# Every third weight tile of an fp32r decoder trunk split by two GpSimd transfers instead of ScalarE and VectorE

## The chip, the core and the metric

The kernel runs on one core of a Trainium2 chip. Its engines are TensorE (PE in the rows; PEld is its weight load), VectorE (DVE), ScalarE (ACT), GpSimd (POOL) and SyncE (SP), with 16 DMA engines beside them. The metric is the device time of one execution in microseconds (us).

## What is computed

A two-layer decoder trunk over 256 tokens of width 1024 in float32. Each layer is a feed-forward block (FFN), a mixer, and a second FFN, each followed by a layer norm. Cut to its core:

```
for l in range(2):
    x = layer_norm(ALPHA*x + 0.5*swiglu(x, ffn_w_gu[l,0], ffn_w_down[l,0]))
    y = mixer_ab(x) if l % 2 == 0 else mixer_c(x)     # attention + gated MLP; mLSTM
    x = layer_norm(ALPHA*x + y)
    x = layer_norm(ALPHA*x + 0.5*swiglu(x, ffn_w_gu[l,1], ffn_w_down[l,1]))

def swiglu(x, w_gu, w_down):
    g, u = split(x @ w_gu, 2)
    return (silu(g) * u) @ w_down
```

FFN widths are 1024 to 2 x 2816 and 2816 back to 1024. Nearly all of the work is products with weights that are used once.

## The kernel before

The weights are packed into 324 tiles of 128 x 1024 float32 (512 KB), numbered in the order of use. Tiles 0 to 65 belong to the first FFN, 66 to 93 to `mixer_ab`, 94 to 159 and 160 to 225 to the second and third FFN, 226 to 257 to `mixer_c`, 258 to 323 to the last FFN. Tiles 0 to 3 come in another way, with x (in_F).

To keep float32 accuracy each operand is a pair: a high part rounded to float32r (`whi`, `xTh`) and a low part, the remainder (`wlo`, `xTl`). `mm3` (lines 119 to 122) multiplies high by high, high by low and low by high into the same PSUM tile.

A weight tile n passes three steps. `w_dma(n)` (line 73) loads it from HBM into one of RAW = 6 `raw` buffers, on SP's queue. `w_split(n)` (line 78) makes `whi` and `wlo`, each a ring of RING = 9 buffers: ScalarE casts `raw` to `whi` (line 92), VectorE subtracts `whi` from `raw` into `wlo` (line 93). Then TensorE uses the pair and `w_done(n)` (line 86) frees it. `w_done(n)` also writes the next steps into the program: `w_split(n + 9)`, whose cast must wait until TensorE has released tile n's buffers, and `w_dma(n + 15)`.

In the FFN, `proj_t` takes one tile per 128 columns of `x @ w_gu`: 24 matmuls of 256 columns into a PSUM bank `ps_m` (3 banks). `chunk` uses two tiles, gate and up: ScalarE's Silu reads the gate bank (line 334), VectorE multiplies with the up bank (line 337), and the product is split again into `hT`. `out_proj` multiplies `hT` with the last 22 tiles of an FFN, in 12 matmuls of 512 columns each, into `ps_a`.

`layer_norm` (line 206) runs on VectorE, except for one small step: GpSimd's power function (line 203, `lnrs`; the same line serves `sgrs` and `hrs` in the mixers). After it VectorE finishes the row block (line 226) and TensorE transposes it (line 234). GpSimd does little else than these powers.

SP's instructions run in the order of the program text. On the other engines a list scheduler chooses the order within an engine when the kernel is built; each engine then works strictly in that order, and an instruction that waits holds up all that stand behind it.

Of the kernel before, what the change touches and what calls it, by code (L numbers as in the profile page):

```python
# [7 lines left out]
F32 = mybir.dt.float32  # L8
# [3 lines left out]
OP = mybir.AluOpType  # L12
# [18 lines left out]
def trunk(ctx, tc, W, F_d, x_d, g_d, b_d, rope_d, id_d, idb_d, mk_d, tri_d, sel_d,  # L31
          sg_d, sb_d, sw_d, sbt_d, cw_d, wif_d, bif_d, hg_d, out_d):
    nc = tc.nc
    NG = W.shape[0] + 4
# [35 lines left out]

    raw, whi, wlo = {}, {}, {}

    def w_dma(n):
        if n < NG:
            raw[n] = wpool.tile([P, 1024], F32, tag="raw", name="raw", bufs=RAW)
            nc.sync.dma_start(out=raw[n], in_=W[n - 4])

    def w_split(n):
        if n < NG:
            hi = wpool.tile([P, 1024], F32R, tag="hi", name="whi", bufs=RING)  # L80
            lo = wpool.tile([P, 1024], F32R, tag="lo", name="wlo", bufs=RING)
            r = raw.pop(n)
            split(r, hi, lo)
            whi[n], wlo[n] = hi, lo

    def w_done(n):
        del whi[n], wlo[n]
        w_split(n + RING)
        w_dma(n + RING + RAW)

    def split(src, hi, lo):
        nc.scalar.copy(out=hi, in_=src)  # L92
        nc.vector.tensor_tensor(out=lo, in0=src, in1=hi.bitcast(F32), op=OP.subtract)  # L93
# [63 lines left out]
    def feed(i):  # L157
        if i < KC:
            st[i] = wpool.tile([P, 1024], F32, tag="raw", name="raw", bufs=RAW)
            eng = nc.scalar if i in (1, 3) else nc.sync  # L160
            eng.dma_start(out=st[i][:, 0:768], in_=F_d[i])
        else:
            w_dma(i - KC + 4)
# [22 lines left out]
    for n in range(4, RING):  # L186
        w_split(n)
        w_dma(n + RAW)
# [669 lines left out]
```

## Time and profile before

| | |
|---|---|
| median of 3 runs | 972.62 us (971.28 to 972.83) |
| profiled execution, its own time | 971.34 us |
| its span in the trace | 969.5 us |
| TensorE busy | 957.2 us, 99% of the span |
| VectorE busy | 599.0 us, 62% |
| ScalarE busy | 458.3 us, 47% |
| GpSimd busy | 25.1 us, 3% |
| SP's DMA queue (q1) | 181.25 MB, 57.4% of the 16 DMA engines' span |

The span lies between the first and the last instruction of the trace; the execution's own time is 1.84 us more. Busy shares are averages over stages with different limits. TensorE's granted clock was 0.999 of full speed.

### The profile page before, as it was taken

The page shows a single profiled execution, that of the slowest core. Times are in us where ns is not written, and L with a number is a line of the kernel's source. Part 1 is how long each engine was busy: PE and PEld are TensorE (multiplying, and loading weights), DVE is VectorE, ACT ScalarE, POOL GpSimd, SP SyncE. Part 2 cuts the span into 40 slices and gives each one's busy share as a digit, 9 for nine tenths or more (in the row PEclk, how much of TensorE's full clock was granted, in tenths as well). Part 3 has the DMA queues.
Part 4 walks back from the last instruction along what each step waited for, and adds up shares of the span by engine and source line. Part 5 has one row for each costly group of instructions (what it writes and reads, how often), then busy time and mean ns, then how long its engine had stood idle before and what let it go on. Part 6 is the DMA issues. An engine that isn't in the chain of part 4 may idle for free.

```text
span 969.5 us, 15552 instructions
## 1 busy us (share of the span) xinstructions
PE 957.2 (99%) x6210; PEld 856.0 (88%) x6210; DVE 599.0 (62%) x829; ACT 458.3 (47%) x669; POOL 25.1 (3%) x36
## 2 busy tenths in 40 slices
PE   8999999999999999999999999999999999999997
PEld 6999988887888999988889999888888789999886
DVE  7665544685777655544775555439767886555435
ACT  6554443446645444443354444325675445445320
POOL 0000000020100000000000000001000000000000
PEclk9999999999999999999999999999999999999999
DMA  9985656474436755656566666556643466665511
GB/s 344 327 273 189 194 177 193 157 273 157 131 130 217 235 182 193 190 183 193 173 225 188 194 183 190 190 157 218 217 125 123 135 218 233 189 194 184 187 44 43
DMA packets 51927, 183.01 MB, mean 189 GB/s; under 512 B 6160, under 2 KB 6544, under 8 KB 51728
## 3 DMA queue, kind: packets, MB, share of 16 engines
q1 hardware_dynamic: 51568, 181.25, 57.4%
q8 instruction: 48, 0.79, 0.3%
q10 hardware_dynamic: 288, 0.79, 0.2%
q14 instruction: 23, 0.19, 0.1%
HBM read 180.97 MB, written 1.05 MB: 188 GB/s over the span
## 4 chain that ended last, share of the span: by engine, by line
PE 70%; DVE 2%; POOL 0%; issue 0%; ACT 0%; DVEq 0%
PE ps_m L120 15%; PE ps_m L121 15%; PE ps_m L122 15%; PE ps_a L121 8%; PE ps_a L122 8%; PE ps_a L120 8%; DVE wlo L93 1%; PE ps_a L234 1%; POOL hrs L203 0%; PE ps_t L323 0%; ACT whi L92 0%; PE ps_a L499 0%; DVE hst L680 0%; DVE num L707 0%; PE ps_a L661 0%
## 5 line engine op out<-in xcount | busy, mean ns | idle before, releaser
L93 DVE TENSOR_TENSOR wlo<-raw,whi 128x1024 fp32r<-128x1024 f32 (+1 forms) x327 | 394.0, 1213 | 232.8 <-ACT whi L92 231.4
L92 ACT CAST whi<-raw 128x1024 fp32r<-128x1024 f32 (+1 forms) x327 | 339.7, 1042 | 380.0 <-PE ps_m L121 194.4
L120 PE MATMUL ps_m<-xTh,whi 128*128 128x256 f32 x1280 | 358.2, 280 | 1.4 <-DVE qkc L647 1.4
L121 PE MATMUL ps_m<-xTl,whi 128*128 128x256 f32 x1280 | 357.6, 279 | 0.0
L122 PE MATMUL ps_m<-xTh,wlo 128*128 128x256 f32 x1280 | 357.4, 279 | 0.0
L120 PEld LDWEIGHTS ps_m<-xTh,whi 128*128 128x128 f32 x1280 | 240.6, 188 | 2.1 <-ACT cch L92 1.6
L121 PEld LDWEIGHTS ps_m<-xTl,whi 128*128 128x128 f32 x1280 | 240.6, 188 | 0.4 <-issue 0.2
L122 PEld LDWEIGHTS ps_m<-xTh,wlo 128*128 128x128 f32 x1280 | 240.6, 188 | 0.3 <-issue 0.3
L121 PE MATMUL ps_a<-wlo,hT 128*128 128x512 f32 (+1 forms) x352 | 138.1, 392 | 0.0
L120 PE MATMUL ps_a<-whi,hT 128*128 128x512 f32 (+1 forms) x352 | 138.1, 392 | 0.0
L122 PE MATMUL ps_a<-whi,hT 128*128 128x512 f32 (+1 forms) x352 | 138.0, 392 | 0.0
L120 PE MATMUL ps_m<-whi,xTh 128*128 128x512 f32 x224 | 90.8, 405 | 0.0
L121 PE MATMUL ps_m<-wlo,xTh 128*128 128x512 f32 x224 | 89.3, 399 | 0.0
L122 PE MATMUL ps_m<-whi,xTl 128*128 128x512 f32 x224 | 88.7, 396 | 0.0
L120 PEld LDWEIGHTS ps_a<-whi,hT 128*128 128x128 f32 x352 | 66.1, 188 | 15.2
L122 PEld LDWEIGHTS ps_a<-whi,hT 128*128 128x128 f32 x352 | 66.1, 188 | 15.1
L121 PEld LDWEIGHTS ps_a<-wlo,hT 128*128 128x128 f32 x352 | 66.2, 188 | 15.0
L337 DVE TENSOR_TENSOR hp<-hp,ps_m 128x256 f32<-128x256 f32 x74 | 31.2, 422 | 52.9 <-PE ps_m L122 52.8
L122 PEld LDWEIGHTS ps_m<-whi,xTl 128*128 128x128 f32 x224 | 42.1, 188 | 9.6
L120 PEld LDWEIGHTS ps_m<-whi,xTh 128*128 128x128 f32 x224 | 42.2, 189 | 8.9
L121 PEld LDWEIGHTS ps_m<-wlo,xTh 128*128 128x128 f32 x224 | 42.2, 188 | 8.7
L212 DVE SCALAR_TENSOR_TENSOR xn<-xn,ps_a 128x512 f32<-128x512 f32 x24 | 16.0, 685 | 37.1 <-PE ps_a L122 37.0
(199 smaller groups left out, 609.2 us busy)
## 6 DMA issues: line engine op xcount, KB each, us to landing
raw<-in_W SPq DMA_DIRECT2D x320, 512.0 KB, 4.0
gb<-in_g SPq DMA_DIRECT2D x6, 512.0 KB, 4.0
gb<-in_b SPq DMA_DIRECT2D x6, 512.0 KB, 4.9
raw<-in_F SPq DMA_DIRECT2D x6, 384.0 KB, 4.2
xn<-in_x SPq DMA_DIRECT2D x1, 1024.0 KB
out<-xn SPq DMA_DIRECT2D x4, 256.0 KB, 2.0
raw<-in_F ACTq DMA_DIRECT2D x2, 384.0 KB, 5.2
swt<-in_sw SPq DMA_DIRECT2D x2, 256.0 KB, 7.4
```

Of the source, the lines that this page charges most:

```text
L92: nc.scalar.copy(out=hi, in_=src)
L93: nc.vector.tensor_tensor(out=lo, in0=src, in1=hi.bitcast(F32), op=OP.subtract)
L120: mm_(out=out, lhsT=lh, rhs=rh, start=start, stop=False)
L121: mm_(out=out, lhsT=lh, rhs=rl, start=False, stop=False)
L122: mm_(out=out, lhsT=ll, rhs=rh, start=False, stop=stop)
L212: nc.vector.scalar_tensor_tensor(out=sl, in0=sl, scalar=scale, in1=acc[i], op0=OP.mult, op1=OP.add)
L234: nc.tensor.transpose(pt[:, c, :], sl[:, c * P:(c + 1) * P], ident)
L337: nc.vector.tensor_tensor(out=hp[:, 1, :], in0=hp[:, 0, :], in1=pu, op=OP.mult)
```

## The change

Tiles n with n >= 12 and n divisible by 3 (104 of the 324) are split in another way. They have no `raw` buffer and no transfer on SP. GpSimd issues a transfer from HBM into `whi` whose destination type is float32r, so that the transfer rounds. ScalarE writes `wlo` = -`whi`. GpSimd then issues a second transfer of the same HBM tile into `wlo` that adds to what is there. VectorE has no part in these tiles.

```diff
+    def viadma(n):
+        return 12 <= n < NG and n % 3 == 0
+
     def w_dma(n):
-        if n < NG:
+        if n < NG and not viadma(n):
             raw[n] = wpool.tile([P, 1024], F32, tag="raw", name="raw", bufs=RAW)
             nc.sync.dma_start(out=raw[n], in_=W[n - 4])
 
     def w_split(n):
         if n < NG:
             hi = wpool.tile([P, 1024], F32R, tag="hi", name="whi", bufs=RING)
             lo = wpool.tile([P, 1024], F32R, tag="lo", name="wlo", bufs=RING)
-            r = raw.pop(n)
-            split(r, hi, lo)
+            if viadma(n):
+                nc.gpsimd.dma_start(out=hi, in_=W[n - 4])
+                nc.scalar.mul(out=lo, in_=hi.bitcast(F32), mul=-1.0)
+                nc.gpsimd.dma_start(out=lo, in_=W[n - 4], accum_op=OP.add)
+            else:
+                r = raw.pop(n)
+                split(r, hi, lo)
             whi[n], wlo[n] = hi, lo
```

How the instructions stand on two engines follows. Line numbers grow by 8 below the edit: 92 becomes 100, 203 becomes 211, 334 becomes 342. A number behind a name counts the buffers handed out; `wlo_1094` and `whi_1093` are one tile, and a higher number is a later tile.

GpSimd, from its set-up to the first two layer norms' powers, before the change:

```order
L138 MEMSET half_82 128x8
L139 MEMSET zero_81 128x256
L203 ISA
L203 TENSOR_TENSOR lnrs_2018<-lnrs_2018,half_82 128x1
L203 TENSOR_TENSOR lnrs_2144<-lnrs_2144,half_82 128x1
L396 MEMSET kp_2100 64x256
```

Nothing stands between the set-up and the powers: GpSimd waits for VectorE and no more.

GpSimd at the end of the first FFN after the change, around the first of these powers (the pairs shown here are the last of many):

```order
L86 DMA whi_1834<-in_W 128x1024
L88 DMA wlo_1835<-in_W 128x1024
L86 DMA whi_1887<-in_W 128x1024
L88 DMA wlo_1888<-in_W 128x1024
L211 ISA
L211 TENSOR_TENSOR lnrs_1994<-lnrs_1994,half_82 128x1
L86 DMA whi_1976<-in_W 128x1024
L86 DMA whi_2025<-in_W 128x1024
L88 DMA wlo_1977<-in_W 128x1024
L88 DMA wlo_2026<-in_W 128x1024
```

Between set-up and power there are now transfers. Those of a tile stand as a pair, high then low, and in the FFN the pairs follow one another strictly: the high part of the next such tile is behind the low part of the one before. A high transfer waits for TensorE's release of the buffer, a low one for ScalarE's negation. The powers now stand behind such pairs.

ScalarE, in the same `chunk` part; before:

```order
L92 CAST whi_901<-raw_701 128x1024
L92 CAST hT_908<-hp_843 128x256
L92 CAST whi_937<-raw_737 128x1024
L334 ACTIVATE hp_911<-ps_m_912 128x256
L92 CAST whi_969<-raw_769 128x1024
L92 CAST hT_976<-hp_911 128x256
```

and after:

```order
L100 CAST whi_1025<-raw_827 128x1024
L87 ACTIVATE wlo_995<-whi_994 128x1024
L100 CAST hT_1032<-hp_968 128x256
L100 CAST whi_1061<-raw_863 128x1024
L342 ACTIVATE hp_1035<-ps_m_1036 128x256
L100 CAST hT_1099<-hp_1035 128x256
L100 CAST whi_1128<-raw_930 128x1024
L87 ACTIVATE wlo_1094<-whi_1093 128x1024
L342 ACTIVATE hp_1102<-ps_m_1103 128x256
```

The negation of a tile (line 87) stands directly behind the cast of the tile after it, once in three tiles, and Silu and the splits of `hT` stand behind the negation.

## Rows read from the trace of the kernel before

**Rows 1.** The page's first part: span, and busy time of the engines.
```profile
span 969.5 us, 15552 instructions
PE 957.2 (99%) x6210; PEld 856.0 (88%) x6210; DVE 599.0 (62%) x829; ACT 458.3 (47%) x669; POOL 25.1 (3%) x36
```

**Rows 2.** TensorE in order of time in the first FFN: start, duration, instruction.
```profile
99.79 0.28 PE L120 MATMUL ps_m<-xTh,whi 128*128 128x256 f32 x1
99.91 0.28 PE L121 MATMUL ps_m<-xTl,whi 128*128 128x256 f32 x1
...
102.59 0.28 PE L120 MATMUL ps_m<-xTh,whi 128*128 128x256 f32 x1
```

**Rows 3.** Busy time by stage: FFN, mixer_ab, mixer_c; then clock, DMA share, GB/s.
```profile
66.60:122.60 56.00, 56.00 (x482) 56.00 (x482) 32.10 (x40) 26.92 (x42) 0.00 (x0) 1.00 0.59 188
191.00:290.00 99.00, 98.70 (x557) 79.51 (x556) 72.83 (x125) 54.88 (x109) 9.02 (x14) 1.00 0.53 176
666.00:770.00 104.00, 101.86 (x578) 86.05 (x577) 77.12 (x153) 57.44 (x90) 7.99 (x8) 1.00 0.47 154
```

**Rows 4.** ScalarE in order of time in the FFN; in brackets idle time before, releaser.
```profile
110.37 1.05 ACT L92 CAST whi<-raw 128x1024 fp32r<-128x1024 f32 x1 [1.44 <-PE ps_m L121]
111.32 0.38 ACT L334 ACTIVATE hp<-ps_m 128x256 f32<-128x256 f32 x1
113.17 1.05 ACT L92 CAST whi<-raw 128x1024 fp32r<-128x1024 f32 x1 [1.47 <-PE ps_m L121]
114.12 0.40 ACT L92 CAST hT<-hp 128x256 fp32r<-128x256 f32 x1
```

**Rows 5.** Groups by line and shape: count, busy us, mean ns, idle before.
```profile
L93 DVE TENSOR_TENSOR wlo<-raw,whi 128x1024 fp32r<-128x1024 f32 x320 | 389.2, 1224 | 232.7 <-ACT whi L92 231.4
L92 ACT CAST whi<-raw 128x1024 fp32r<-128x1024 f32 x320 | 335.4, 1051 | 380.0 <-PE ps_m L121 194.4 <-PE ps_a L122 149.9 <-PE ps_m L122 21.6
L203 POOL TENSOR_TENSOR lnrs<-lnrs,half 128x1 f32<-128x1 f32 x12 | 11.4, 951 | 803.0 <-DVE lnrs L202 789.3 <-DMA raw<-in_W 13.7
L203 POOL TENSOR_TENSOR hrs<-hrs,half 128x2 f32<-128x2 f32 x4 | 4.6, 1152 | 80.9 <-DVE hrs L202 80.9
L203 POOL TENSOR_TENSOR sgrs<-sgrs,half 128x1 f32<-128x1 f32 x2 | 3.1, 1554 | 52.1 <-DVE sgrs L202 52.1
```

**Rows 6.** The tile raw from 66 to 123 us: issue in ns, time to landing.
```profile
L76 SPq DMA_DIRECT2D raw<-in_W x20: 327/328/328, 67.9 to 121.1; - x20
...
DMA to landing us min/median/max: 3.3/3.5/4.2
```

**Rows 7.** The page's third part: SP's queue, packets, MB, share of 16 engines.
```profile
q1 hardware_dynamic: 51568, 181.25, 57.4%
```

**Rows 8.** Who waited for whom: total us, times, longest us.
```profile
PEld ps_a L234 <- DVE xn L226: 1.3, 6, 0.3
DVE hrs L701 <- POOL hrs L203: 2.8, 4, 0.8
```

## Prediction

> **What bounds the kernel now.** I read the busy times first. TensorE is busy for 957.2 of 969.5 us [rows 1], so at most 12.3 us of the span are not matmuls, whatever is done to the other engines. TensorE's own instructions are the same after the change, so these 12.3 us bound every gain. Next, in order of time, TensorE in an FFN: 24 matmuls of 256 columns lie between 99.79 and 102.59 us [rows 2], so one weight tile takes 2.80 us and three take 8.40. In the FFN window TensorE is never idle, while the DMA engines are used for 0.59 of the time at 188 GB/s [rows 3]. ScalarE shows who leads: each cast of a tile starts after an idle time of 1.44 us that ends when TensorE releases the buffer [rows 4]. The splitting keeps up easily; it runs at TensorE's pace with nine tiles, 25.2 us, from the release of a buffer to the next use.
>
> **The change part by part.** *Removed:* 104 subtractions on VectorE, 1.224 us each [rows 5], 127 us of an engine that TensorE does not wait for in the FFN: worth nothing there. In the mixers TensorE idles for 0.30 us of 99 and 2.14 us of 104 [rows 3], where VectorE is busier; freeing it can give back 2.4 us at most. I take 0.
>
> *Replaced:* 104 casts on ScalarE become 104 negations of the same size. No row shows the negation; its nearest row is the cast, 1.051 us [rows 5]. The bound below is Silu's 0.38 us for a quarter of the elements [rows 4], which would leave the sum nearly as it is. I take 1.05, so ScalarE's load stays.
>
> *Moved and added:* 104 raw transfers leave SP and 208 transfers of 512 KB appear on GpSimd. This is where the time is decided, because of the order on GpSimd and ScalarE. For one tile: GpSimd waits for the release, issues the high transfer, ScalarE waits for it to land, negates, GpSimd issues the low transfer, and only then, in GpSimd's order, can the high transfer of the next such tile be issued. That is a loop, and TensorE offers it 8.40 us per turn in an FFN. If the loop is longer, the ring's lead runs out and TensorE goes at the loop's pace.
>
> The loop's terms. (a) Issue on GpSimd, once for each transfer. Not shown: from below SP's issue, 0.33 us [rows 6]; from above GpSimd's longest mean for its own tiny instruction, 1.55 us [rows 5]. GpSimd takes 0.95 us even for 128 x 1 elements [rows 5], and I take 0.93, close to that: two issues are 1.9 us. (b) The high transfer from issue to landing. SP's take 3.3 to 4.2 us, median 3.5 [rows 6]. Of this the bytes are 1.65 us: 188 GB/s at a share of 0.59 is 319 GB/s at full use [rows 3], and a tile is 0.524 MB. Whether a rounding transfer is slower is not shown; below one pass, above two. I take one, 3.5 us. (c) The low transfer must read its destination as well as HBM. Bounds: one pass, 1.65 us, if the second read is free, and three, 4.95. I take two, 3.3 us of engine time. It was issued just before the next high transfer on the same queue, so that one stands behind it for 3.3 - 0.93 = 2.4 us. (d) Two raw transfers per loop, 3.3 us of the DMA engines, share them. The GpSimd transfers hold the engines for 4.95 us of a loop of some 10.5; the part of the raw work that falls into it is 3.3 x 4.95 / 10.5 = 1.6 us. (e) Negation 1.05 and two hand-overs, 0.1 together. Sum: 1.9 + 3.5 + 2.4 + 1.6 + 1.15 = 10.5 us against 8.40. That is 2.1 us per turn.
>
> No run here shows the price of an accumulating transfer. The Trainium skill, Collectives: The Full Stack, section The bandwidth ceiling: the fold count and why AG ≠ RS ≠ AR, says that an add inside a transfer halves its rate, because it needs two source reads and not because of the adding; by that (c) would be two passes.
>
> The four FFNs hold 84 such tiles (18 in the first, 22 in each other): 84 x 2.1 = 176 us. The lead absorbs some of it once: 25.2 us less a tile's unhindered way of 0.93 + 3.5 + 1.15 + 0.93 + 3.5 + 1.65 = 11.7 leaves 13.5 us. In the mixers three tiles take 99 / 28 x 3 = 10.6 us and 104 / 32 x 3 = 9.75 us [rows 3], so a loop of 10.5 neither costs nor rebuilds the lead in the first, and costs ten turns x 0.75 = 7.5 us in the second. 176 - 13.5 + 7.5 = 170 us.
>
> *The powers on GpSimd:* 18 of them [rows 5] now stand behind transfers that wait. Six transposes arrived at TensorE with only 0.2 us of waiting each [rows 8], that is, with no room left; VectorE in mixer_c waits for `hrs` already, 2.8 us in four [rows 8]. A power can be late by nothing, or by one high transfer, negation and issue, 0.93 + 3.5 + 1.15 = 5.6 us. At 2 us each that is 36 us; where TensorE waits for tiles anyway most of it lies under that, and I take 10.
>
> *Behind the waiting negation on ScalarE* stands Silu. TensorE needs that PSUM bank again two tiles, 5.6 us, after filling it. The negation stands behind the next tile's cast, at 2.8 + 1.05 = 3.9 us after the release; with an unhindered landing after 4.4 us this costs nothing, with 6.8 us (with the wait behind the low transfer) Silu still makes it. The loop binds first.
>
> *DMA engines:* SP's 57.4% [rows 7] lose 104 x 0.524 = 54.5 of 181.25 MB, 17.3 points; the high transfers put 17.3 back and the low ones add 34.5: 92% of the old span, 892 us, so bandwidth alone is not the bound.
>
> The profiled execution took 971.3 us: 971.3 + 170 + 10 = 1151; the median of the runs is 1.3 higher: 1152 us.
>
> **The rivals.** *Hidden (15%).* If the low transfer costs one pass and the issue 0.33 us, the loop is 0.66 + 3.5 + 1.3 + 1.3 + 1.15 = 7.9 us, below 8.40, and TensorE never notices: 971 to 975 us. TensorE's 99% and the 41% of free DMA time speak for it [rows 1, 3]; it decides at 8.40. The Trainium skill, DMA: Bandwidth & Descriptors, section Anatomy of one DMA — SWDGE (gpsimd) path, fits a GpSimd transfer as 2.0 us plus its bytes at 436 GB/s; that estimate gives 3.2 us for a tile, issue and landing together, and would bring the hidden case. No row of this trace has a transfer from GpSimd.
>
> *The loop fits, the powers are late (12%).* 18 x 1 to 2 us on top: 990 to 1010 us. For it speak the transposes without room [rows 8].
>
> *Transfers that compute are slow (12%).* With three passes for the low and two for the high one, and 1.55 us for an issue, (a) to (e) give 3.1 + 5.15 + 3.4 + 1.9 + 1.15 = 14.7 us: 84 x 6.3 plus about 90 in the mixers, less the lead, some 600 us more: 1580. Against it speaks only that nothing shows it.
>
> *Faster (6%).* VectorE without a third of its subtractions lets TensorE's 2.4 us of waits in the mixers go: 969 to 970 us. This needs a loop under 8.40 us and powers on time.
>
> **How the numbers follow.** The loop as summed has 55%. Its own range is from a loop just over 8.40 us, with the powers late, 1000 us, to three passes for the low transfer: (c) 4.0, (d) 2.0, loop 12.5, 84 x 4.1 + 46 - 13 = 377 us, 1350. For 8 in 10 the range must also hold the hidden case: 971 to 1400 leaves out the faster case and the slow transfers, 18%. A measurement of this kernel tells some 0.2%, 2 us, from no change; so faster has 6%, the same 15%, slower 79%.
>
> **What would show it.** In the changed profile: GpSimd's queue alternating high and low transfers at more than 8.4 us a pair in the FFN; ScalarE's negation waiting for the high transfer; TensorE waiting for `wlo` of the GpSimd tiles; VectorE 127 us less busy; 235 MB read from HBM. The prediction is wrong if the pairs keep 8.40 us, which the landing times of the GpSimd transfers decide: high under 4.7 us after the wait on GpSimd ends.

## The result, and the profile after

The changed kernel takes 1103.58 us (median of 4 runs, 1092.16 to 1112.83) against 972.73 us of the kernel before on the same chip: 1.131 times as long, interval 1.127 to 1.135. That is slower by 131 us, where 179 were forecast. The profiled execution happens to be the longest of the four runs (1112.83 us at a granted clock of 0.96, against 0.964 to 0.972 in the others), so its trace shows a loss of 142 us and not of 131.

The first part of the changed kernel's page, which answers to [rows 1]:

```profile
span 1111.1 us, 15612 instructions
PE 1002.9 (90%) x6210; PEld 884.5 (80%) x6210; DVE 479.9 (43%) x725; ACT 449.4 (40%) x669; POOL 167.9 (15%) x244
```

TensorE still has its 6210 matmuls, but two things grew. Its idle time, span less busy time, went from 12.3 to 108.2 us, and its busy time from 957.2 to 1002.9 us. VectorE lost 119 us and idles more; it was never the bound.

Busy time by stage, as in [rows 3], in four stretches: most of the first FFN, its end with `mixer_ab`, and the chunk parts of the second and third FFN. After the stretch's length come PE, PEld, DVE, ACT and POOL, then clock, DMA share and GB/s:

```profile
60.00:190.00 130.00, 119.93 (x810) 110.05 (x808) 44.60 (x56) 50.72 (x70) 19.78 (x28) 0.99 0.78 225
190.00:300.00 110.00, 97.78 (x529) 78.12 (x530) 60.24 (x108) 52.12 (x104) 20.55 (x32) 0.94 0.72 205
330.00:440.00 110.00, 96.77 (x690) 89.99 (x689) 46.25 (x65) 44.57 (x66) 16.20 (x23) 0.97 0.77 220
520.00:640.00 120.00, 104.83 (x668) 93.35 (x667) 52.00 (x74) 46.08 (x66) 17.94 (x27) 0.96 0.76 219
```

No stretch is spared, in none of the four are the DMA engines full in the mean, and the clock lies below 1.00 where TensorE idles. A finer cut tells the places apart. The next three rows sum the four stretches in which TensorE works on the `chunk` parts of the FFNs, from their first matmul to their last: in the kernel before, in the changed kernel, and in run 1 (below). First comes the length of the four together.

```profile
sum 415.30, PE 415.30 PEld 415.24 DVE 247.81 ACT 205.77 POOL 0.00; mean PE 103.83 PEld 103.81 DVE 61.95 ACT 51.44 POOL 0.00
sum 461.40, PE 429.98 PEld 424.40 DVE 186.73 ACT 201.21 POOL 70.93; mean PE 107.50 PEld 106.10 DVE 46.68 ACT 50.30 POOL 17.73
sum 423.50, PE 419.04 PEld 418.59 DVE 187.85 ACT 206.23 POOL 71.66; mean PE 104.76 PEld 104.65 DVE 46.96 ACT 51.56 POOL 17.92
```

So of the 142 us that this execution lost, 46 lie in the chunk parts and 96 outside them. Of the 96, the two stretches with a mixer, each from the end of one chunk part to the start of the next, hold 35 and 37.

The queues, as in [rows 7]; q0 is GpSimd's:

```profile
q0 software_dynamic: 29952, 109.07, 42.6%
q1 hardware_dynamic: 36592, 126.72, 30.8%
...
HBM read 235.49 MB, written 1.05 MB: 213 GB/s over the span
```

What TensorE waited for (total us, times, longest us), against nothing of the kind before:

```profile
PE ps_a L129 <- DMA wlo<-in_W: 28.4, 8, 6.2
PE ps_m L128 <- ACT hp L342: 23.1, 18, 4.9
PE ps_m L129 <- DMA wlo<-in_W: 21.6, 8, 4.4
```

It waits for the low parts of GpSimd tiles, and, which the prediction had at nothing, for Silu (line 342, the matmul that needs Silu's PSUM bank again). The time from issue to landing of the 104 high parts, as in [rows 6]:

```profile
DMA to landing us min/median/max: 3.8/7.0/11.9
```

GpSimd and then ScalarE in order of time in the first FFN; in brackets the idle time before and what ended it:

```profile
94.01 0.84 POOL L88 DMA_DIRECT2D wlo<-in_W  x1 [6.76 <-ACT hT L100]
94.80 0.62 POOL L86 DMA_DIRECT2D whi<-in_W  x1
102.57 0.85 POOL L88 DMA_DIRECT2D wlo<-in_W  x1 [7.16 <-ACT hp L342]
103.28 0.71 POOL L86 DMA_DIRECT2D whi<-in_W  x1
111.47 0.85 POOL L88 DMA_DIRECT2D wlo<-in_W  x1 [7.48 <-ACT hT L100]
```

```profile
101.22 1.06 ACT L87 ACTIVATE wlo<-whi 128x1024 fp32r<-128x1024 f32 x1 [2.81 <-DMA whi<-in_W]
102.18 0.36 ACT L342 ACTIVATE hp<-ps_m 128x256 f32<-128x256 f32 x1
...
110.11 1.06 ACT L87 ACTIVATE wlo<-whi 128x1024 fp32r<-128x1024 f32 x1 [3.22 <-DMA whi<-in_W]
```

This is the predicted loop, and GpSimd has no slack in it: each high part here is issued right behind a low part (94.80), with no wait for TensorE's release. ScalarE waits 2.8 to 3.2 us until it lands, negates (101.22 to 102.28), and the low part follows at 102.57. A turn takes 8.56 us here and 8.90 the next time. From the first low part to the last of the tiles away from the blocks' ends, the mean turn in the four FFNs is 9.26, 9.37, 8.90 and 8.84 us (11 turns in the first, from tile 24 on, then 13 each). TensorE offers 8.40. Silu stands behind the held negation.

### The profile page after: what moved, and what is told of

It reads as the page before. It is cut to its first block, busy times and chain, and to the rows that moved or that the text cites. A ratio compares the mean times of both kernels' runs of the same rounds, so it can differ in the third digit from the quotient of the medians.

```text
span 1111.1 us, 15612 instructions
## 1 busy us (share of the span) xinstructions
PE 1002.9 (90%) x6210; PEld 884.5 (80%) x6210; DVE 479.9 (43%) x725; ACT 449.4 (40%) x669; POOL 167.9 (15%) x244
## 3 DMA queue, kind: packets, MB, share of 16 engines
HBM read 235.49 MB, written 1.05 MB: 213 GB/s over the span
## 4 chain that ended last, share of the span: by engine, by line
issue 50%; DMA 22%; PE 13%; POOL 10%; DVE 2%; ACT 1%; SPq 0%; POOLq 0%; DVEq 0%; ACTq 0%
DMA whi<-in_W 19%; POOL wlo L88 5%; POOL whi L86 4%; PE ps_m L128 2%; PE ps_m L129 2%; PE ps_m L130 2%; DMA wlo<-in_W 2%; PE ps_a L129 2%; PE ps_a L130 1%; PE ps_a L128 1%; PE ps_m L363 1%; DMA swt<-in_sw 1%; ACT hT L100 1%; POOL lnrs L211 1%; DVE wlo L101 1%
## 5 line engine op out<-in xcount | busy, mean ns | idle before, releaser
L128 PE MATMUL ps_m<-xTh,whi 128*128 128x256 f32 x1280 | 365.3, 285 | 23.9 <-ACT hp L342 23.1
L101 DVE TENSOR_TENSOR wlo<-raw,whi 128x1024 fp32r<-128x1024 f32 (+1 forms) x223 | 266.6, 1206 | 231.6 <-ACT whi L100 230.9
L100 ACT CAST whi<-raw 128x1024 fp32r<-128x1024 f32 (+1 forms) x223 | 228.7, 1032 | 139.0 <-PE ps_a L130 66.9
L87 ACT ACTIVATE wlo<-whi 128x1024 fp32r<-128x1024 f32 x104 | 110.2, 1060 | 367.6 <-DMA whi<-in_W 361.2
L88 POOL DMA_DIRECT2D wlo<-in_W x104 | 89.2, 857 | 658.2 <-ACT wlo L87 266.6
L129 PE MATMUL ps_a<-wlo,hT 128*128 128x512 f32 (+1 forms) x352 | 142.7, 406 | 24.2 <-DMA wlo<-in_W 24.2
L128 PE MATMUL ps_a<-whi,hT 128*128 128x512 f32 (+1 forms) x352 | 141.8, 403 | 1.8 <-DMA whi<-in_W 1.8
L130 PE MATMUL ps_a<-whi,hT 128*128 128x512 f32 (+1 forms) x352 | 141.5, 402 | 0.0
L86 POOL DMA_DIRECT2D whi<-in_W x104 | 77.5, 745 | 214.2 <-PE ps_m L130 109.1
L128 PEld LDWEIGHTS ps_a<-whi,hT 128*128 128x128 f32 x352 | 68.4, 194 | 18.5 <-DMA whi<-in_W 2.7
L130 PEld LDWEIGHTS ps_a<-whi,hT 128*128 128x128 f32 x352 | 68.4, 194 | 15.6
L101 DVE TENSOR_TENSOR hT<-hp,hT 128x256 fp32r<-128x256 f32 x74 | 31.3, 423 | 98.8 <-ACT hT L100 98.8
```

The source lines that it names most:

```text
L86: nc.gpsimd.dma_start(out=hi, in_=W[n - 4])
L87: nc.scalar.mul(out=lo, in_=hi.bitcast(F32), mul=-1.0)
L88: nc.gpsimd.dma_start(out=lo, in_=W[n - 4], accum_op=OP.add)
L128: mm_(out=out, lhsT=lh, rhs=rh, start=start, stop=False)
L129: mm_(out=out, lhsT=lh, rhs=rl, start=False, stop=False)
L130: mm_(out=out, lhsT=ll, rhs=rh, start=False, stop=stop)
```

## The experiments

The theories, in the words of the expectations: **T1**, the loop on GpSimd; **T2**, the traffic of the DMA engines; **T3**, ScalarE held by the negation that waits, so that Silu is late; and, after the first four runs, **T4**, a second place that loses, the block boundaries, and **T5**, late powers. Each kernel is compared with the kernel before on its own chip (971.4 to 972.5 us).

**1. The high part ahead.** On GpSimd the high part of the next such tile is issued ahead of the low part of the one before, and the negation stands one cast later. Where blocks meet, `w_low(0)` first finishes the tile that is still open (these calls are not shown):

```diff
-                nc.gpsimd.dma_start(out=hi, in_=W[n - 4])
-                nc.scalar.mul(out=lo, in_=hi.bitcast(F32), mul=-1.0)
-                nc.gpsimd.dma_start(out=lo, in_=W[n - 4], accum_op=OP.add)
+                last["hi"] = nc.gpsimd.dma_start(out=hi, in_=W[n - 4]).ins
+                late.append((n, hi, lo))
...
+            w_low(1)
...
+    def w_low(keep):
+        while len(late) > keep:
+            n, hi, lo = late.pop(0)
+            with tc.issue_after(last["cast"]):
+                nc.scalar.mul(out=lo, in_=hi.bitcast(F32), mul=-1.0)
+            with tc.issue_after(last["hi"]):
+                nc.gpsimd.dma_start(out=lo, in_=W[n - 4], accum_op=OP.add)
```

> Same transfers, same bytes, same tiles; only the order differs: on GpSimd the high transfer of the next tile stands ahead of the low transfer of the one before, and ScalarE's negation stands one cast later. Theory 1 (the loop high transfer, negation, low transfer, next high transfer on GpSimd is longer than the 8.40 us that TensorE needs for three tiles): the loop is cut, so 970 to 985 us. Theory 2 (the added traffic on the DMA engines slows the loads): the traffic is unchanged, so 1080 to 1115 us. Theory 3 (ScalarE, held by the negation, is late with Silu and so with the PSUM banks): mended too, 970 to 1000 us.

1041.59 us, ratio 1.071 (1.066 to 1.076), in no theory's range. Its windows in the chunk part of the second FFN, and at the end of the first with `mixer_ab`:

```profile
190.00:300.00 110.00, 96.32 (x535) 76.45 (x534) 61.29 (x111) 53.73 (x107) 21.01 (x32) 0.98 0.70 196
...
330.00:440.00 110.00, 110.00 (x894) 107.62 (x893) 50.70 (x70) 55.44 (x82) 19.16 (x27) 1.00 0.94 261
```

In this chunk part TensorE is never idle again, with the DMA engines used for 0.94 of the time, and a turn takes 8.40 us, TensorE's own pace. So the order of these instructions was the cause there. In the whole kernel it was worth 61 of the 131 us, but not in the chunk parts alone: between the two profiled executions, 79 us apart, the chunk parts account for 38 us (461.4 to 423.5) and the rest of the kernel for 41. Some 70 us remain, nearly all outside the chunk parts (55 of the 63 us that this trace is still longer than the one before): a second cause.

**2. Every fourth tile.** `n % 4 == 0` in place of `n % 3`, 78 tiles.

> Every fourth tile instead of every third. Theory 1: TensorE now offers the loop 11.2 us a turn, more than the 9 us that pairs take in the changed kernel, so the loss nearly goes: 973 to 990 us. Theories 2 and 3: three quarters of the transfers and of the waiting negations, so about three quarters of the 131 us: 1060 to 1080 us.

1065.96 us, ratio 1.098 (1.095 to 1.102): per tile as dear as before (1.2 us), although TensorE now offers 11.2 us a turn. The stretch from 330 to 440 us, what TensorE waited for, and GpSimd in order of time:

```profile
PE ps_m L128 <- ACT hp L342: 5.6, 7, 2.2
```

```profile
388.64 0.55 POOL L86 DMA_DIRECT2D whi<-in_W  x1 [2.42 <-PE ps_m L130]
397.42 0.86 POOL L88 DMA_DIRECT2D wlo<-in_W  x1 [8.23 <-ACT hp L342]
```

GpSimd has slack here: it waits 2.42 us for TensorE's release before it issues the high part. TensorE still loses 5.6 us, all of it to Silu behind the held negation. T3 exists by itself, beside the loop, and the expectation of theory 1 is missed.

**3. No add.** The low transfer overwrites instead of adding (`accum_op` left out). The low part of these tiles is left out by this: `wlo` receives the tile itself.

> The low transfer overwrites instead of adding, so the low part is left out (it holds the rounded weight); the number of transfers and every wait stay. Theory 1 with a low transfer of two passes: one pass of 1.65 us less in front of the next high transfer, the loop comes to 7.3 to 7.8 us, below 8.40: 973 to 995 us. If the addition costs nothing the time stays at 1095 to 1110 us. Theory 2: less engine time by 104 passes of 1.65 us, 172 us of 1100, some 1030 to 1070 us. Theory 3: about as theory 1.

1021.37 us, ratio 1.051 (1.049 to 1.053), between the ranges of the theories. The mean turn falls to 8.1 to 8.7 us, and the chunk parts lose 12 us in the profiled execution instead of 46; the other 37 of its 49 us lie outside them. So the add was worth 81 us, more than half of it outside the chunk parts. It lengthens the low transfer, and the high transfer behind it lands after 5.4 us in the median instead of 7.0.

**4. The negation on VectorE.**

```diff
-                nc.scalar.mul(out=lo, in_=hi.bitcast(F32), mul=-1.0)
+                nc.vector.tensor_scalar(out=lo, in0=hi.bitcast(F32), scalar1=-1.0, scalar2=None, op0=OP.mult)
```

> The negation on VectorE instead of ScalarE, all else as in the changed kernel. Theory 1: the loop has the same members, so the loss stays for the most part: 1050 to 1110 us, with pairs on GpSimd still at 8.8 to 9.2 us. Theory 3: ScalarE never waits for a transfer, Silu is on time, so 970 to 1000 us, unless VectorE's product behind the negation is late in its stead.

1235.84 us, ratio 1.272 (1.268 to 1.275), twice the loss, which neither theory had in its range. TensorE's two longest waits:

```profile
PE ps_m L128 <- DVE hp L345: 74.5, 26, 4.7
PE ps_a L129 <- DMA wlo<-in_W: 58.9, 21, 6.5
```

The held queue is now VectorE's. Behind the negation stand the products that free PSUM banks and the subtractions of the other tiles, and the mean turn grows to 11.1 to 11.4 us (from the second FFN on). By its share in the changed profile VectorE is hardly busier than ScalarE (43% against 40%), and it is the far worse place.

The remaining runs separate the places. "Inner" tiles are the 58 GpSimd tiles of the chunk parts, away from the blocks' ends; the other 46 lie at block boundaries and in the mixers.

```diff
     def viadma(n):
-        return 12 <= n < NG and n % 3 == 0
+        inner = 12 <= n < 59 or any(f + 17 <= n < f + 59 for f in (94, 160, 258))
+        return inner and n % 3 == 0
```

**5 and 6. Inner tiles only; boundary and mixer tiles only** (the same with `not inner`, from tile 59 on).

> The 58 GpSimd tiles that lie inside the FFNs' chunk part stay; the 46 at block boundaries and in the mixers go back to the old way. Theory T4 (two places lose: inside the FFNs the loop on GpSimd turns in about 9.1 us against TensorE's 8.4, and at the boundaries a tile has some 11 us from release to use, less than its own way): 58 turns x 0.7 = 40 us less what each stretch's lead absorbs (up to 13 us in each of four), so 15 to 40 us over before, 988 to 1012 us, with TensorE's waits for wlo and Silu inside the FFNs and none at the boundaries. Rival T2 (the traffic of the DMA engines costs, wherever the tiles lie): 58/104 of 131 us, 73 us: about 1045 us. Rival T5 (the powers behind transfers cost most of it): the powers here have no transfers around them, so nearly nothing is lost: 971 to 980 us.

> The reverse: the 46 GpSimd tiles at the block boundaries and in the mixers stay, the 58 inside the chunk parts go back. T4: most of the loss stays, 70 to 105 us over before, 1040 to 1075 us, TensorE waiting for wlo in ps_a at each boundary; together the two halves lose about what the whole change does. T2: 46/104 of 131 us: 58 us, about 1030 us. T5: nearly the whole loss, 1090 us and above, with TensorE's waits at the transposes behind xn and msp and not at weight tiles.

Inner: 1000.33 us, ratio 1.029 (1.025 to 1.034). Boundary: 1042.63 us, 1.072 (1.067 to 1.076). What TensorE waited for, first with the inner tiles, then with the others:

```profile
PE ps_m L129 <- ACT hp L343: 18.0, 12, 4.9
```

```profile
PE ps_m L130 <- DMA wlo<-in_W: 18.5, 8, 3.7
PE ps_a L130 <- DMA wlo<-in_W: 14.2, 4, 5.4
```

The two lose 28 and 70 us, together 98 of the 131. The missing 33 lie mostly outside the chunk parts: there the changed kernel's profiled execution loses 96 us, run 6's 64 and run 5's nothing, while the chunk parts lose 46 against 10 and 26. So the places are not independent: boundary tiles cost more where a chunk part with GpSimd tiles goes before them. That the loop leaves them no lead would explain it; no run shows that by itself. T2 as a price of bytes fails: 58 tiles cost 28 us and 46 cost 70. With inner tiles only, TensorE waits for Silu and hardly for tiles (18.0 us in 12 waits): the loop makes each high part later than the one before, until the negation that waits for it holds Silu.

**7. Inner tiles, high part ahead** (1 and 5 together).

> Inner tiles only, and on GpSimd the high transfer of the next tile stands ahead of the low one of the tile before, the negation one cast later. T4: the loop is gone and no tile lies at a boundary, so nothing is left to lose: 971 to 978 us. T2: the same bytes as with the inner tiles in the old order, about 1045 us. T5: 971 to 980 us, as for the inner tiles in the old order.

976.15 us, ratio 1.004 (1.003 to 1.006), with 3.4 us of it a single wait for a low part.

**8 and 9. The two halves of that reorder.** Inner tiles only. First, GpSimd as in the changed kernel, but the negation behind the cast of tile n + 2. Then the high part ahead on GpSimd, but the negation behind the cast of tile n + 1, where the changed kernel has it. The second edit, against the changed kernel:

```diff
+            if late and n - late[0][0] in (1, 3):
+                m, hi, lo = late[0]
+                if n - m == 1:
+                    with tc.issue_after(last["cast"]):
+                        nc.scalar.mul(out=lo, in_=hi.bitcast(F32), mul=-1.0)
+                else:
+                    late.pop(0)
+                    with tc.issue_after(last["hi"]):
+                        nc.gpsimd.dma_start(out=lo, in_=W[m - 4], accum_op=OP.add)
```

> Inner tiles only, GpSimd in the changed order (low part of a tile, then high part of the next), but the negation stands one cast later on ScalarE, so that less of ScalarE's work waits behind it. If the loop on GpSimd is what loses in the chunk part (T1), nothing is won, since the negation comes no earlier: 995 to 1005 us, as with the inner tiles in the old order (1000). If ScalarE, held by the negation that waits for its transfer, is the loss (T3: there TensorE waited for Silu and not for tiles), it goes: 972 to 980 us.

> The other half: inner tiles only, on GpSimd the high transfer of the next tile ahead of the low one of the tile before, but the negation directly behind the next cast, as in the changed kernel. T1: the loop is opened, so the loss goes: 972 to 980 us. T3: the high transfer is issued at the release, some 4 us before the negation's turn, and lands 5 to 7 us after its issue, so ScalarE is still held 1 to 3 us once in three tiles and some of the Silu waits stay: 980 to 995 us.

The later negation alone: 989.15 us, ratio 1.019 (1.015 to 1.023), between the two expectations. Silu's waits fall from 18.0 to 9.8 us, but now TensorE waits 8.5 us for low parts: the turn is still 8.6 to 9.7 us. The high part ahead alone: 973.37 us, ratio 1.001 (1.000 to 1.002), no difference that this measurement can tell. GpSimd in that kernel:

```profile
95.95 0.54 POOL L87 DMA_DIRECT2D whi<-in_W  x1 [6.97 <-PE ps_m L142]
96.48 0.90 POOL L101 DMA_DIRECT2D wlo<-in_W  x1
104.35 0.54 POOL L87 DMA_DIRECT2D whi<-in_W  x1 [6.97 <-PE ps_m L142]
```

GpSimd now idles 7 us a turn until TensorE releases a buffer, and the turn is 8.40 us. The high part leaves at the release, so ScalarE's waits fall too: 84.6 us in all, against 194.0 with the inner tiles in the changed order. With every third tile the loop was the cause in the chunk part, and the hold of ScalarE mostly its consequence; run 2 shows that the hold can cost without the loop.

**10. No negation.** All 104 tiles, two plain transfers, the second independent of the first. The low part is left out, as in 3, and 235.49 MB are read as in the changed kernel.

```diff
                 nc.gpsimd.dma_start(out=hi, in_=W[n - 4])
-                nc.scalar.mul(out=lo, in_=hi.bitcast(F32), mul=-1.0)
-                nc.gpsimd.dma_start(out=lo, in_=W[n - 4], accum_op=OP.add)
+                nc.gpsimd.dma_start(out=lo, in_=W[n - 4])
```

> All 104 tiles, but no negation and no add: two plain transfers fill whi and wlo, the second independent of the first (the low part is left out: wlo gets the tile itself). It moves as many bytes as the run whose low transfer overwrites, and only the chain high transfer, negation, low transfer is taken away. T4: a tile's way is then two issues and one landing, about 7 us, below the 8.4 of a turn and below the 11 of a boundary: 971 to 990 us. T2: as in that run, about 1021 us. T5: the powers still stand among transfers, but these now wait for releases alone: about 980 to 1000 us.

981.23 us, ratio 1.009 (1.007 to 1.010). Its page:

```profile
span 980.4 us, 15405 instructions
PE 959.7 (98%) x6210; PEld 858.6 (88%) x6210; DVE 479.7 (49%) x725; ACT 355.5 (36%) x565; POOL 132.8 (14%) x244
```

So 208 transfers from GpSimd with the bytes of the changed kernel cost 9 us in all, the powers among them included, and 4.5 of those are one wait for a late layer norm. Against run 3, which moves the same bytes, the chain high, negation, low is worth 41 us; with it went the 104 negations, some 110 us of ScalarE's time, which this run does not price apart. Bytes by themselves (T2) are not what loses.

**11. Boundary and mixer tiles, every sixth** (23 tiles, `n % 6`).

> Boundary and mixer tiles only, every sixth instead of every third (23 of the 46). T4 (where tiles are released 1.4 us apart, three tiles come every 4.2 us and a turn takes 9, so the second such tile is late): with 8.4 us between two such tiles most of the loss goes, 975 to 995 us. T2 or any fixed price for each tile: half of the 70 us that the 46 lost: about 1007 us.

1002.38 us, ratio 1.031 (1.027 to 1.035): a miss. 30 us for 23 tiles are 1.3 us each, against 1.5 for the 46; rarer tiles are hardly cheaper. It is not their spacing. One tile of this run, on GpSimd and then on TensorE:

```profile
483.09 0.55 POOL L87 DMA_DIRECT2D whi<-in_W  x1 [18.20 <-DVE lnmv L227]
...
488.36 0.89 POOL L89 DMA_DIRECT2D wlo<-in_W  x1 [4.00 <-ACT wlo L88]
```

```profile
496.24 0.50 PE L130 MATMUL ps_m<-wlo,xTh 128*128 128x512 f32 x1 [1.21 <-DMA wlo<-in_W]
```

A single tile, with no other GpSimd transfer before it, is on its way from 483.09 to 496.24 us, 13.1 us, and TensorE stood ready 1.21 us sooner. The high part landed after 3.8 us, the low one only after 7.8. SP issues four `raw` transfers for the same burst between 487.08 and 492.01 us, and the DMA engines are used for 0.95 to 0.96 of the time while the low part is under way:

```profile
488.30:492.30 4.00, 4.00 (x21) 3.22 (x21) 3.27 (x4) 3.56 (x5) 0.90 (x2) 1.00 0.95 243
492.30:496.20 3.90, 2.72 (x12) 1.87 (x10) 3.87 (x7) 0.00 (x0) 0.55 (x1) 1.00 0.96 264
```

The low parts of the changed kernel land after 5.4 us in the median, so the burst's own traffic very likely makes the chain longer at this place; no run separates that part of T2. What the kernel before has there shows why the ring gives no more. ScalarE's casts at the end of the second FFN, each at a release; TensorE's first matmul of the third FFN (`ps_m`) stands at 477.24 us in the same trace:

```profile
457.57 1.05 ACT L92 CAST whi<-raw 128x1024 fp32r<-128x1024 f32 x1 [1.75 <-PE ps_a L122]
468.70 1.05 ACT L92 CAST whi<-raw 128x1024 fp32r<-128x1024 f32 x1 [10.08 <-PE ps_a L122]
470.08 1.06 ACT L92 CAST whi<-raw 128x1024 fp32r<-128x1024 f32 x1 [0.33 <-PE ps_a L122]
```

`out_proj` first goes over its last seven tiles for one half of the tokens and releases nothing (457.57 to 468.70); then it releases one every 1.4 us. The next block starts its tiles 1.4 us apart too, because it also takes the halves of the tokens in turn. The tile loaded into the buffer released at 468.70 is the third of the next block (tile 162), needed at about 477.24 + 2 x 1.4 = 480.0: 11.3 us from release to use, where the chunk part gives 25.2.

**12. Late powers, without any transfer on GpSimd.** The kernel before, with eight additions of zero behind each power.

```diff
         nc.gpsimd.tensor_tensor(out=r, in0=r, in1=half[:, :width], op=OP.pow)
+        for _ in range(8):
+            nc.gpsimd.tensor_tensor(out=r, in0=r, in1=zero[:, :width], op=OP.add)
```

> The kernel before, without any transfer on GpSimd, but each power is followed by eight additions of zero on GpSimd, 5 to 7 us, so that each layer norm ends later. It prices two things. If late powers were a large part of the loss, a delay of 5 to 7 us on each of 18 costs 60 us or more (1030 us and above). If idle time of TensorE by itself lowers the granted clock, TensorE's busy time rises above 957 us by some 0.3 to 0.5 us for each us of added idle time, with no transfer involved; if transfers were what slowed the matmuls, busy time stays at 957.

1002.66 us, ratio 1.031 (1.030 to 1.033). Its page:

```profile
span 1000.6 us, 15690 instructions
PE 966.0 (97%) x6210; PEld 860.3 (86%) x6210; DVE 600.0 (60%) x829; ACT 458.4 (46%) x669; POOL 67.8 (7%) x180
```

The additions took 0.30 us each, (67.8 - 25.1) / 144, so a power came 2.4 us late and not 5 to 7. VectorE then waits 32.9 us for these additions' results, and the kernel loses 30.3 us: late powers do cost nearly what VectorE waits for them. In the changed kernel VectorE waits 14.3 us for `lnrs` (4 times), which by this rate is an estimate of 13 us. By that estimate T5 is a part, and not the large one.

## Why the prediction was right, and where it was not

**Right: the loop is real, in its place.** It was forecast from the order of instructions and is in the trace: high and low in strict turn, 8.8 to 9.4 us against 8.40, ScalarE's negation waiting for the high part, TensorE for `wlo`, VectorE 119 us less busy, 235 MB. With the inner tiles alone, opening the order wins 27 of the 28 us (run 9 against run 5); in the whole kernel it wins 61 (run 1), by the traces about half of it in the chunk parts.

**Wrong in size: the loop's sum, 10.5 us.** By the rows, a turn is 0.79 us from low to high issue, 6.42 from there until ScalarE starts, and 1.35 for negation and hand-over: 8.56. Three terms were too large. (a) the step from a low to a high issue was taken at 0.93 and took 0.54 to 0.79. (b) counted the high part's issue twice: SP's 3.5 us to landing are counted from the issue, and its own 0.93 us had been added in (a). (c) the low transfer was taken as two passes. GpSimd's queue was busy for 0.426 x 1111.1 = 473 us in the changed kernel and, without the add, for 0.340 x 1018.6 = 346 us, 1.67 us a transfer. If the high ones cost the same in both, a low one is (473 - 104 x 1.67) / 104 = 2.88 us, 1.7 passes. The rounding costs nothing that shows, as assumed: 1.67 us stands against 1.65 for a plain tile.

The Trainium skill (Collectives: The Full Stack, The bandwidth ceiling: the fold count and why AG ≠ RS ≠ AR) says of a ReduceScatter that its add needs two source reads, which halves the rate. Carried over to this transfer it comes out a little high: two passes against 1.7, by that estimate.

The 58 inner tiles at the measured mean of 9.1 us a turn give 58 x 0.7 = 41 us; the chunk parts of the profiled execution lost 46, in which the clock and the waits for Silu are too. The forecast had 58 x 2.1 - 13.5 = 108 for them.

**Wrong: the lead of 25.2 us from release to use, taken for every stage.** This step failed, and it hid the larger part of the loss. The lead was read in the chunk part and never held against the boundaries. At the boundary between two FFNs a tile has 11.3 us from release to use, and its way took 13.1 even with no other GpSimd transfer before it (unhindered it was estimated at 11.7). The prediction counted the 26 tiles at the FFNs' ends as turns of the loop like the others (26 x 2.1 = 55 us) and gave the 20 in the mixers 7.5. These 62 us stand near the 70 that the 46 tiles cost alone (run 6), but that is luck, since the mechanism is another: outside the chunk parts run 1's open order still leaves 55 of the 96 us, while run 10, where the chain is gone (negation and add with it), leaves 11.

**Wrong: "Silu still makes it".** TensorE waited 23.1 us for Silu. The sum took the negation at 3.9 us after the release and the landing after 6.8; it left out that in a loop too long each high part leaves later after its release than the one before it. Nor does it need the loop: in run 2 GpSimd waits for the release, and Silu is late all the same.

**Missing: the clock.** No term had it. TensorE's busy time grew by 45.7 us with the same matmuls, a third of the profiled loss (below).

**The powers** had 10 us; run 12's rate makes it an estimate of 13.

So the time fell near the forecast partly because errors of opposite sign met. Against the profiled execution's 142 us, the chunk parts were forecast 62 us too dear (108 against 46) and the rest, powers included, 24 too cheap (72 against 96); the clock was left out of both. That bandwidth alone is not the bound held (run 10). The hidden rival failed at its own condition, a landing under 4.7 us: the median high part landed after 7.0, ahead of which stands a low part. The Trainium skill's fit (DMA: Bandwidth & Descriptors, Anatomy of one DMA — SWDGE (gpsimd) path) gave an estimate of 3.2 us; the shortest here is 3.8 and, in run 10, where nothing adds, the median of the high parts is 5.5. No landing in these runs is as short, and the estimate spoke for the wrong case.

**What stays open.** How the 70 us at the boundaries divide between a tile's own way, the burst's traffic, ScalarE held by the negation and late powers was not separated; in run 6 TensorE's waits for low parts are 36.1 us of the 48.8 us of idle time that it added. Nor was a longer ring tried. No version beat the kernel before: the best, run 9, equals it and frees VectorE of 69 us of work that nobody waits for.

## What to carry to other kernels

A transfer that depends on an earlier transfer through an engine makes a chain of two landings, and every in-order queue that it touches (GpSimd, ScalarE) is held for it; issue the next tile's first transfer ahead of the last one's second. Measure the time from a buffer's release to its use in each stage, above all where blocks meet and buffers come free in bursts, and hold it against the way of one tile. Price a stall of TensorE at more than its length, because the clock falls behind it.

## What the runs showed of the hardware

**Idle time of TensorE costs 1.3 to 1.5 times itself in these kernels.** In run 6 TensorE waits 5.10 us for a low part. Windows before the wait, in it, just after it, and then:

```profile
486.00:492.00 6.00, 6.00 (x27) 4.71 (x26) 1.23 (x1) 1.29 (x3) 0.00 (x0) 1.00 0.86 296
492.00:497.30 5.30, 0.27 (x2) 0.00 (x0) 1.22 (x1) 0.84 (x1) 0.85 (x1) 0.81 0.70 134
497.30:502.20 4.90, 4.83 (x11) 3.80 (x12) 1.38 (x2) 0.00 (x0) 0.00 (x0) 0.51 0.18 73
502.20:506.00 3.80, 3.80 (x18) 3.08 (x17) 0.77 (x2) 0.00 (x0) 0.00 (x0) 1.00 0.00 0
```

For 4.9 us after the gap the granted clock is 0.51, the lower level of 1.2 GHz, and matmuls that took 0.23 us take 0.43; then it is 2.4 GHz again. Over the runs the busy time grows with the idle time by much the same share:

| kernel | idle time of TensorE, added us | busy time, added us | ratio |
|---|---|---|---|
| run 12, no transfer on GpSimd | 22.3 | 8.8 | 0.39 |
| run 1 | 45.7 | 17.3 | 0.38 |
| run 6 | 48.8 | 25.2 | 0.52 |
| changed kernel | 95.9 | 45.7 | 0.48 |
| run 4 | 178.3 | 87.2 | 0.49 |

The other runs that added more than 8 us of idle time lie between 0.30 (run 10) and 0.52 (run 2). Run 12 has no more traffic than the kernel before, so it takes no added transfer to slow the matmuls; idle time is enough.

**Issuing costs GpSimd 0.54 us for a transfer** where neither adds (run 10: 55.7 us for 104 of each kind). In the changed kernel the adding ones take 0.857 in the mean and the high ones 0.745, up to 0.88 where one stands right behind an adding one. All are below the 0.95 us of one tiny power [rows 5], and above SP's 0.33 [rows 6].
